# Second token group: stretches without gathers, fewer gathers in its layers, and ten row buffers with the products eight slots behind

## The chip, the cores and the metric

The kernel runs on one core of a Trainium2 chip, as one launch. The metric is the device time of that core in microseconds (us), the median of several runs; lower is better. TensorE is called PE here, VectorE DVE, ScalarE ACT, GpSimd POOL and SyncE SP; each has an instruction queue of its own and works it off in order. A gather is a DMA that POOL issues: it fetches 128 rows of a table, one for each partition, by row numbers that lie in SBUF.

## The reference

512 tokens of width 1024 pass through five layers in a row: a Mamba2 mixer, a sliding-window attention (SWA), a hybrid of gated delta rule and mLSTM, a cross attention to 256 memory tokens, and a PEER expert layer. In the expert layer each token picks, for each of 8 heads, 16 of 16,384 experts; an expert is one row of a table `u` and one row of a table `v`:

```python
q = (hf @ wq).reshape(t, PEER_HEADS, 2, PEER_HALF)
sc = jnp.einsum('thpd,hpnd->thpn', q, sub_keys).astype(jnp.float32)
...
u = jnp.take(u_table, eb, axis=0)
act = jax.nn.gelu(jnp.einsum('phkd,pd->phk', u, xb).astype(jnp.float32), approximate=False)
wgt = (gb * act).astype(v_table.dtype)
return jnp.einsum('phk,phkd->pd', wgt, jnp.take(v_table, eb, axis=0))
```

The layers between the mixers carry matrix products of 1024 by up to 6176, all in float32. Residuals and a last normalization close the chain. Mamba, SWA, the delta rule and the mLSTM go along the tokens, so later tokens need the state of earlier ones.

## The kernel before

The tokens are worked in two groups of 256 (two blocks of 128 each), one group after the other through all layers (`layers`). The expert layer is done in two ways. For the first group the 128 chosen experts of each token are fetched: 2 blocks x 2 tables x 128 slots are 512 gathers of 512 KB each (class `Rows`, line 1928 on). For the second group all 16,384 experts are computed densely on PE in 128 steps (`steps`), each step with a 512 KB tile of the `u` table and one of the `v` table, until the `u` tiles run out after step 93. The dense steps are called the steady expert part below.

The 512 gathers belong to the first group but are not done at its end. They are a side stream, a Python generator (`after`), which `run` (line 1885 on) draws on while it writes down the second group's layers: after each piece of a layer an account grows by a rate of that layer (`RATE`: 1.0 in mamba, 1.1 in SWA, hybrid and cross, 0.5 in the routing), and for each whole unit `Rows.next` writes one gather into the program. What is left when the second group's layers and routing are written goes evenly into the steps of the steady expert part (`steps`, `left`).

`Rows.next` allocates one of 6 row buffers (`gu`), issues the gather on POOL and, once more than `GLAG` = 5 gathers are pending (3 in the steady part), writes the oldest one's product (`take`): one DVE pass over 128x1024 elements, for a `u` row a product with the token that is summed up (L1969), for a `v` row a scaled addition to the output `x` (L1975). A gather thus waits for the product of the gather six before it. `behind` ties each gather and each product, in the order alone, behind the matmul written last.

The order in the queues is a scheduler's. The side stream has a lower priority (-300), and so gathers and products slip to where their engines would be free by the scheduler's reckoning, or pile up behind more urgent work.

Each layer ends alike. The output projection's second half (`out_part`, last=True) is evacuated by DVE (L646), its squares are summed on ACT, mamba and SWA then scale and add (`post`, L607 to L615), and the next layer's `norm_T` needs a power on POOL (L460), a scaling on DVE (L500) and transposes on PE (L412) before the next layer's first matmul can start. Mamba's state update in each chunk goes from POOL (L816) to DVE (L817) to PE. In the hybrid layer `finish` normalizes the heads' output on DVE, ACT and POOL (L1361 to L1378) before it is transposed (`outT`) and projected.

In the second group the weights of these layers are used as float32 as they come (`FULL`), so that the tile `hl` and the tile `ol`, which hold low parts of activations for the first group, have no user in the second group's layers up to the dense part.

Of the kernel before, what the change touches and what calls it, by code (L numbers as in the profile page):

```python
# [9 lines left out]
F32 = mybir.dt.float32  # L10
# [10 lines left out]
D = 1024  # L21
# [125 lines left out]
SPLIT_R = [V]  # L147
SPLIT_D = [V]
SPLIT = {"A": SPLIT_A, "B": SPLIT_B, "R": SPLIT_R, "G": SPLIT_D, "D": SPLIT_D}
RB = 1.0  # L150
RR = 0.5
RT = 1.793
RBS = 1.1
RBH = 1.1
RBX = 1.1
RG = 0.5
RATE = {"A": 0.0, "T": RT, "B": RB, "R": RR, "G": RG, "swa": RBS, "hybrid": RBH, "cross": RBX}
RAWB = 3
# [1 line left out]
GBUF = 6  # L160
HP = 99
WV = (2, 3)
GLAG = 5
GLEAD = 2
GD = 2.9
GU = 0.6
# [20 lines left out]
class Kern:  # L187
    PD = 2

    def __init__(self, ctx, tc, a, out, groups, stop=None):  # L190
# [12 lines left out]
        self.phase = "A"  # L203
        self.tail = None
        self.rows = None
        self.hook = None
        self.tab = ("", [], [])
        self.push("op")
# [271 lines left out]
    def norm_T(self, x, nb, wcol, keep=None, halo=None, ss=None, full=False, dst=None):  # L480
# [4 lines left out]
        with self.tc.high_priority(HP):  # L485
            for b in range(nb):
# [10 lines left out]
                r = self.rstd(s1, 1, "n", 1.0 / D)  # L497
# [7 lines left out]
        with self.tc.high_priority(HP):  # L505
            for k in range(8):
                p = self.ps([128, gt], "tp")
                for b in range(nb):
                    self.tr(p[:, b * 128:(b + 1) * 128], xn[b][:, k * 128:(k + 1) * 128])
                nc.scalar.activation(hh[:, k, :], p, AF.Copy, scale=wcol[:, k:k + 1])  # L510
                if full:
                    continue
                nc.vector.scalar_tensor_tensor(hl[:, k, :], p, wcol[:, k:k + 1], hh[:, k, :].bitcast(F32),
                                               op0=ALU.mult, op1=ALU.subtract)
        if keep is not None:
            for b in range(nb):
                nc.gpsimd.tensor_tensor(keep[0][:, b, :], xn[b], keep[1], op=ALU.mult)
# [100 lines left out]
    def out_part(self, key, oT, nb, kh, k0, evac, last=False, done=None):  # L618
# [8 lines left out]
                yield  # L627
        if last:
            us = [self.W((key, kh, c)) for c in (2, 3)]
            for b in range(nb):  # L630
                for c in (2, 3):
                    p = self.ps([128, 256], "mm")
                    self.n_half(p, us[c - 2], oT, b, k0, True, True)
                    evac(b, c, p)
                    yield
                if done is not None:
                    done(b)
# [403 lines left out]
    def hybrid(self, gi, x, nb):  # L1041
# [317 lines left out]
        oT = self.oT(gt, self.is_full(gi, "ho"))  # L1359

        def finish(b, f0):  # L1361
            fs = slice(f0, f0 + 4)
            if f0 == 4:
                ab = self.sb([128, 4], "dab")
# [33 lines left out]
        yield from self.weave_keep(g_proj("h_z", 0, AF.Silu), side, 2.0)  # L1398
        yield from self.weave(side, ml, 0.5)
        yield from outT(4)  # L1400
        if gi == 0:
            yield from self.memory_kv(2, "cacc", 3)
        fin = chain(*[finish(b, 0) for b in range(nb)], outT(0))
        yield from self.weave(self.out_part("h_o", oT, nb, 1, 4, self.acc_evac(xs)), fin, 1.0)
        self.xss = self.pp.tile([128, nb, 4], F32, name="xss", tag="xss", bufs=2)
        yield from self.out_part("h_o", oT, nb, 0, 0, self.end_evac(xs, self.xss, "P"), last=True)
        if gi == 0:
# [480 lines left out]
    def run(self):  # L1888
# [5 lines left out]
        for gi, (b0, nb) in enumerate(self.groups):  # L1894
            x = self.load_x(gi) if gi else x0
            acc = 0.0
            for _ in self.layers(gi, x, nb):
# [1 line left out]
                if ph == "B" and self.layer in RATE:  # L1899
                    ph = self.layer  # L1900
                acc = min(3.0, acc + RATE[ph])
                while side is not None and acc >= 1:
                    acc -= 1
                    with self.tc.high_priority(GOFF[self.phase] if self.tail is None else TOFF):
                        if next(side, 0) == 0:
                            side = None
# [11 lines left out]
    def after(self, gi, x, nb):  # L1918
# [1 line left out]
        self.tail = None  # L1920
        self.rows = Rows(self, gi, x, nb, self.routed)
        while self.rows.seq:
            self.rows.next(GLAG)
            yield
        self.rows.drain()

# [1 line left out]
class Rows:  # L1928
# [9 lines left out]
    def next(self, lag):  # L1938
# [4 lines left out]
                self.ends.pop(0)  # L1943
        if self.seq:
            b, v, s = self.seq.pop(0)
            t = k.gp.tile([128, D], F32, name="gu", tag="gu", bufs=GBUF)
            table = k.a["p_v" if v else "p_u"]
            self.behind(k.nc.gpsimd.indirect_dma_start(out=t, out_offset=None, in_=table,  # L1948
                                                       in_offset=bass.IndirectOffsetOnAxis(ap=self.res[b][0][:, s:s + 1], axis=0)))
            self.pend.append((b, v, s, t))  # L1950
            if len(self.pend) > lag:
                self.take()
        elif self.pend:
            self.take()

    def behind(self, inst):

# [101 lines left out]
```

## Time and profile before

| what | value |
|---|---|
| median of 3 runs | 2544.5 us (2540.04 to 2547.29) |
| the profiled execution | 2548.39 us, its span 2546.6 us |
| mean granted PE clock, share of full | 0.963 |
| busy PE / DVE / ACT / POOL | 2351.7 / 1983.7 / 1182.3 / 1086.4 us |
| bytes moved by DMA | 642.33 MB, of them 268.47 MB by gathers |

The profile page gives the busy time of each engine over the whole span; the answers to questions to the trace, in the section of rows below, cut it into stretches, and list single instructions with the idle time before them and what ended it (in brackets, "<-"). The granted clock is a share of full speed: 1.00 is 2.4 GHz, 0.5 is 1.2 GHz, and what lies between is a mean over both. The second group's layers run from about 780 to 1640 us, the gathers start at 834 us, routing and the making of the gate matrix follow, and the steady expert part runs from 1893 to 2517 us, with `u` and `v` tiles until 2424 us.

### The profile page before, as it was taken

The page shows a single profiled execution, that of the slowest core. Times are in us where ns is not written, and L with a number is a line of the kernel's source. Part 1 is how long each engine was busy: PE and PEld are TensorE (multiplying, and loading weights), DVE is VectorE, ACT ScalarE, POOL GpSimd, SP SyncE. Part 2 cuts the span into 40 slices and gives each one's busy share as a digit, 9 for nine tenths or more (in the row PEclk, how much of TensorE's full clock was granted, in tenths as well). Part 3 has the DMA queues.
Part 4 walks back from the last instruction along what each step waited for, and adds up shares of the span by engine and source line. Part 5 has one row for each costly group of instructions (what it writes and reads, how often), then busy time and mean ns, then how long its engine had stood idle before and what let it go on. Part 6 is the DMA issues. An engine that isn't in the chain of part 4 may idle for free.

```text
span 2546.6 us, 41073 instructions
## 1 busy us (share of the span) xinstructions
PE 2351.7 (92%) x14872; PEld 2119.6 (83%) x14872; DVE 1983.7 (78%) x3978; ACT 1182.3 (46%) x2450; POOL 1086.4 (43%) x910
## 2 busy tenths in 40 slices
PE   7999998999988989979889967999999999999997
PEld 7999898998888878867768856787999999999974
DVE  7777667757579887877779777699878888888876
ACT  6766566645455433423243222224775444444443
POOL 1111101222010677663648775521225655666663
PEclk9999999999999989989979978999999999999999
DMA  6555534324445899987978769876988898898884
GB/s 205 182 171 156 158 105 151 113 90 128 157 141 173 326 371 342 362 282 258 359 277 285 272 223 393 329 255 207 306 265 321 327 343 307 328 337 324 313 290 157
DMA packets 203962, 642.33 MB, mean 252 GB/s; under 512 B 21104, under 2 KB 53360, under 8 KB 202480
## 3 DMA queue, kind: packets, MB, share of 16 engines
q1 hardware_dynamic: 97216, 347.19, 40.0%
q0 software_dynamic: 73728, 268.47, 29.1%
q10 hardware_dynamic: 32816, 24.06, 3.0%
q8 instruction: 117, 1.92, 0.3%
q14 instruction: 85, 0.70, 0.1%
HBM read 621.74 MB, written 17.89 MB: 251 GB/s over the span
## 4 chain that ended last, share of the span: by engine, by line
PE 61%; DVE 15%; issue 8%; POOL 7%; DMA 5%; ACT 4%; ACTq 0%; POOLq 0%; DVEq 0%; SPq 0%
PE mm L404 37%; PE ax L404 18%; POOL gu L1948 4%; PE tp L404 4%; PE tp L412 3%; DMA gu<-in_p_v,eid 2%; DVE wlo L379 2%; DVE x L1975 2%; DVE cacc L532 1%; DMA gu<-in_p_u,eid 1%; DVE gu L1969 1%; ACT whi L376 1%; DVE wk L1524 1%; DMA gd<-gst 1%; DVE ti L1526 1%
## 5 line engine op out<-in xcount | busy, mean ns | idle before, releaser
L379 DVE TENSOR_TENSOR wlo<-wraw,whi 128x1024 fp32r<-128x1024 f32 x285 | 355.9, 1250 | 170.0 <-ACT whi L376 169.8
L1948 POOL DMA_INDIRECT gu<-in_p_v,eid x256 | 384.2, 1501 | 145.1 <-DVE x L1975 68.6
L1948 POOL DMA_INDIRECT gu<-in_p_u,eid x256 | 312.8, 1222 | 305.9 <-DVE gu L1969 205.4
L404 PE MATMUL mm<-hl,whi 128*128 128x256 f32 (+1 forms) x1376 | 391.6, 285 | 0.0
L376 ACT CAST whi<-wraw 128x1024 fp32r<-128x1024 f32 x285 | 298.9, 1050 | 180.6 <-PE mm L404 85.0
L1975 DVE SCALAR_TENSOR_TENSOR x<-gu,act,x 128x1024 f32<-128x1024 f32 x256 | 341.4, 1333 | 17.1 <-DMA gu<-in_p_v,eid 15.4
L1969 DVE SCALAR_TENSOR_TENSOR gu<-gu,hf 128x1024 f32<-128x1024 f32 x256 | 320.4, 1264 | 33.7 <-DMA gu<-in_p_u,eid 33.3
L404 PE MATMUL mm<-hh,whi 128*128 128x260 f32 (+1 forms) x1232 | 331.4, 343 | 2.7 <-DVE spp L563 1.5
L404 PE MATMUL mm<-hh,wlo 128*128 128x260 f32 (+1 forms) x1200 | 322.7, 340 | 3.9 <-DVE wlo L379 3.9
L404 PEld LDWEIGHTS mm<-hl,whi 128*128 128x128 f32 x1376 | 262.6, 191 | 5.0
L404 PEld LDWEIGHTS mm<-hh,whi 128*128 128x128 f32 x1232 | 235.2, 194 | 21.6 <-ACT hh L510 2.8
L1811 POOL TENSOR_TENSOR w<-act,w 128x256 fp32r<-128x256 f32 x128 | 147.2, 1150 | 240.8 <-issue 181.2
L404 PEld LDWEIGHTS mm<-hh,wlo 128*128 128x128 f32 x1200 | 232.4, 197 | 20.8 <-DVE wlo L379 4.7
L404 PE MATMUL mm<-dhh,wlo 128*128 128x256 f32 x752 | 211.5, 281 | 0.0
L404 PE MATMUL mm<-dhh,whi 128*128 128x256 f32 x752 | 209.8, 279 | 0.0
L404 PE MATMUL mm<-wlo,hh 128*128 128x256 f32 x656 | 176.0, 328 | 0.0
L404 PE MATMUL mm<-whi,hh 128*128 128x256 f32 x608 | 166.8, 328 | 0.4 <-ACT hh L510 0.4
L404 PE MATMUL mm<-whi,oh 128*128 128x256 f32 x560 | 147.4, 327 | 1.7 <-DVE ysb L646 1.1
L1806 ACT CAST w<-act 128x256 fp32r<-128x256 f32 x128 | 52.1, 407 | 208.2 <-DVE act L1804 206.2
L404 PE MATMUL mm<-hh,wraw 128*128 128x256 f32 (+1 forms) x608 | 147.3, 389 | 0.3 <-ACT act L1706 0.3
L404 PEld LDWEIGHTS mm<-dhh,whi 128*128 128x128 f32 x752 | 141.1, 188 | 4.0
L404 PEld LDWEIGHTS mm<-dhh,wlo 128*128 128x128 f32 x752 | 141.2, 188 | 0.0
(494 smaller groups left out, 5610.7 us busy)
## 6 DMA issues: line engine op xcount, KB each, us to landing
wraw<-in_w SPq DMA_DIRECT2D x238, 512.0 KB, 3.8
wraw<-in_p_v SPq DMA_DIRECT2D x78, 512.0 KB, 5.3
wraw<-in_p_ut SPq DMA_DIRECT2D x69, 512.0 KB, 4.7
whi<-in_w SPq DMA_DIRECT2D x55, 512.0 KB, 6.5
wlo<-in_w SPq DMA_DIRECT2D x55, 512.0 KB, 5.9
wrawd<-in_p_v SPq DMA_DIRECT2D x50, 512.0 KB, 5.3
wrawd<-in_p_ut SPq DMA_DIRECT2D x36, 512.0 KB, 4.6
gd<-gst ACTq DMA_DIRECT2D x32, 384.0 KB, 4.9
```

The lines of the kernel that those rows point to most:

```text
L376: nc.scalar.copy(hi, raw)
L379: (nc.gpsimd if le == "P" else nc.vector).tensor_tensor(lo, raw, hi.bitcast(F32), op=ALU.subtract)
L404: inst = self.last = self.nc.tensor.matmul(out, lhsT, rhs, start=start, stop=stop, skip_group_check=True)
L412: return self.nc.tensor.transpose(out, in_, self.ident[:in_.shape[0], :in_.shape[0]])
L532: nc.vector.scalar_tensor_tensor(acc, ps[:, 1 + j:1 + j + gt], w[:, j:j + 1], acc, op0=ALU.mult, op1=ALU.add)
L1524: nc.vector.match_replace(work, ov[:, 0:8], vals, -3.0e38)
L1526: nc.vector.max_index(oi[:, 8:16], ov[:, 8:16], work)
L1806: nc.scalar.copy(wt[:, 0:gt], act)
L1811: nc.gpsimd.tensor_tensor(wt[:, gt:2 * gt], act, wt[:, 0:gt].bitcast(F32), op=ALU.subtract)
L1948: self.behind(k.nc.gpsimd.indirect_dma_start(out=t, out_offset=None, in_=table, in_offset=bass.IndirectOffsetOnAxis(ap=self.res[b][0][:, s ...
L1969: self.behind(nc.vector.scalar_tensor_tensor(t, t, 1.0, self.hf[:, b, :], op0=ALU.mult, op1=ALU.mult, accum_out=acts[b][:, s:s + 1]))
L1975: self.behind(nc.vector.scalar_tensor_tensor(x[:, b, :], t, acts[b][:, s:s + 1], x[:, b, :], op0=ALU.mult, op1=ALU.add))
```

## The change

Three edits act on the side stream, and only while the second group's layers are written.

1. **Quiet stretches.** A flag stops `run` from drawing on the side stream. It is set at the last two column tiles of each layer's output projection and taken back in the next layer's `norm_T`; in the hybrid layer also from the first `finish` to the end of `outT(4)`, and again through the first half of the output projection. The account does not grow beyond 3 meanwhile.
2. **Rates.** Mamba 0.95 for 1.0, SWA 1.15 for 1.1, hybrid 1.05 for 1.1, cross 0.95 for 1.1. What the layers issue less goes to the steady expert part.
3. **Ten row buffers, products eight slots behind.** Four more rows are held in the idle tiles `hl` and `ol`, two in each, and `GLAG` = 5 becomes `DEEP` = 8 in the layers. In the routing it is 5 again, and the first call there takes the surplus.

```diff
-RB = 1.0
+RB = 0.95
...
-RBS = 1.1
-RBH = 1.1
-RBX = 1.1
+RBS = 1.15
+RBH = 1.05
+RBX = 0.95
...
+DEEP = 8
...
         self.rows = None
+        self.quiet = False
         self.hook = None
...
                                                op0=ALU.mult, op1=ALU.subtract)
+        self.quiet = False
         if keep is not None:
...
         if last:
             us = [self.W((key, kh, c)) for c in (2, 3)]
+            self.quiet = True
             for b in range(nb):
...
         def finish(b, f0):
+            self.quiet = gi > 0
             fs = slice(f0, f0 + 4)
...
         yield from outT(4)
+        self.quiet = False
         if gi == 0:
             yield from self.memory_kv(2, "cacc", 3)
         fin = chain(*[finish(b, 0) for b in range(nb)], outT(0))
         yield from self.weave(self.out_part("h_o", oT, nb, 1, 4, self.acc_evac(xs)), fin, 1.0)
+        self.quiet = False
...
-                while side is not None and acc >= 1:
+                while side is not None and acc >= 1 and not (self.quiet and ph != "T"):
...
-            self.rows.next(GLAG)
+            self.rows.next(DEEP if self.phase == "B" else GLAG)
...
-            t = k.gp.tile([128, D], F32, name="gu", tag="gu", bufs=GBUF)
+            t = self.buf()
...
-            if len(self.pend) > lag:
+            while len(self.pend) > lag:
                 self.take()
...
+    def buf(self):
+        k = self.k
+        r = k.rot("rb", GBUF + 4) if k.phase == "B" else 0
+        if r < GBUF:
+            return k.gp.tile([128, D], F32, name="gu", tag="gu", bufs=GBUF)
+        if r % 2 == 0:
+            if r == GBUF:
+                self.pair = k.hp.tile([128, 2, D], F32, name="hl", tag="hl")
+            else:
+                self.pair = k.op_tile([128, 2, D], "ol", "ol")
+        return self.pair[:, r % 2, :]
```

What this does to the queues stands below at three places. A row is a source line, an operation, its output, its inputs, the shape, and a count where rows follow each other alike. The changed file's lines lie a little lower: L460 is L462 there, L650 is L654, L646 is L650, L1948 is L1955, L1969 is L1989.

POOL's queue at the end of mamba, before. `ysb` is the projected output, `pr` and `nr` are the powers for the two normalizations, the DMA rows are gathers:

```order
L650 TENSOR_TENSOR ysb<-ysb,bcw 128x256 x2
L1948 DMA gu<-in_p_u,eid 128x1024
L650 TENSOR_TENSOR ysb<-ysb,bcw 128x256
L1948 DMA gu<-in_p_u,eid 128x1024
L650 TENSOR_TENSOR ysb<-ysb,bcw 128x256
L1948 DMA gu<-in_p_u,eid 128x1024 x4
L460 TENSOR_TENSOR pr<-pv,mhalf 128x1 x2
L913 MEMSET va 128x780
L915 COPY kT<-a_kc 128x4x128
L916 COPY va<-a_vc 128x260
L460 TENSOR_TENSOR nr<-nv,mhalf 128x1 x2
```

The same place on POOL in the changed kernel:

```order
L654 TENSOR_TENSOR ysb<-ysb,bcw 128x256
L1955 DMA gu<-in_p_u,eid 128x1024
L654 TENSOR_TENSOR ysb<-ysb,bcw 128x256
L1955 DMA gu<-in_p_u,eid 128x1024
L654 TENSOR_TENSOR ysb<-ysb,bcw 128x256 x2
L462 TENSOR_TENSOR pr<-pv,mhalf 128x1 x2
L917 MEMSET va 128x780
L919 COPY kT<-a_kc 128x4x128
L920 COPY va<-a_vc 128x260
L462 TENSOR_TENSOR nr<-nv,mhalf 128x1 x2
```

The four gathers ahead of `pr` are gone, and one between the `ysb` rows.

DVE's queue at the end of the hybrid layer, before. The rows `gu,act<-gu,hf` are products of gathered rows, `x<-mm,x` is an evacuation, `ns`, `nv` and `xn` are the cross layer's normalization:

```order
L1969 SCALAR_TENSOR_TENSOR gu,act<-gu,hf 128x1024
L646 TENSOR_TENSOR x<-mm,x 128x256
L1969 SCALAR_TENSOR_TENSOR gu,act<-gu,hf 128x1024
L646 TENSOR_TENSOR x<-mm,x 128x256
L1969 SCALAR_TENSOR_TENSOR gu,act<-gu,hf 128x1024
L496 TENSOR_REDUCE ns_15326<-xss 128x1
L496 TENSOR_REDUCE ns_15335<-xss 128x1
L1969 SCALAR_TENSOR_TENSOR gu,act<-gu,hf 128x1024
L458 TENSOR_SCALAR nv<-ns_15326 128x1
L458 TENSOR_SCALAR nv<-ns_15335 128x1
L1969 SCALAR_TENSOR_TENSOR gu,act<-gu,hf 128x1024
L500 TENSOR_SCALAR xn<-x,nr 128x512 x4
```

The same place on DVE in the changed kernel (`hl` and `ol` are now gathered rows too, L1871 is the last normalization of the first group's first block):

```order
L1989 SCALAR_TENSOR_TENSOR hl,act<-hl,hf 128x1024
L650 TENSOR_TENSOR x<-mm,x 128x256
L1989 SCALAR_TENSOR_TENSOR ol,act<-ol,hf 128x1024 x2
L650 TENSOR_TENSOR x<-mm,x 128x256
L1871 SCALAR_TENSOR_TENSOR gu<-x,finr,gu 128x1024
L650 TENSOR_TENSOR x<-mm,x 128x256 x3
L498 TENSOR_REDUCE ns_15183<-xss 128x1
L498 TENSOR_REDUCE ns_15192<-xss 128x1
L460 TENSOR_SCALAR nv<-ns_15183 128x1
L460 TENSOR_SCALAR nv<-ns_15192 128x1
L502 TENSOR_SCALAR xn<-x,nr 128x512 x4
```

Between the last evacuation and `xn` no product is left. Some products still stand among the evacuations ahead of it.

POOL's queue in the steady expert part, before (`w` is one dense step's weighting, one row for each step):

```order
L1811 TENSOR_TENSOR w<-act,w 128x256
L1948 DMA gu<-in_p_v,eid 128x1024
L1811 TENSOR_TENSOR w<-act,w 128x256
L1948 DMA gu<-in_p_v,eid 128x1024
L1811 TENSOR_TENSOR w<-act,w 128x256
L1948 DMA gu<-in_p_v,eid 128x1024 x2
L1811 TENSOR_TENSOR w<-act,w 128x256
```

The same part in the changed kernel:

```order
L1818 TENSOR_TENSOR w<-act,w 128x256
L1955 DMA gu<-in_p_u,eid 128x1024 x2
L1818 TENSOR_TENSOR w<-act,w 128x256
L1955 DMA gu<-in_p_u,eid 128x1024
L1818 TENSOR_TENSOR w<-act,w 128x256
L1955 DMA gu<-in_p_u,eid 128x1024 x2
L1818 TENSOR_TENSOR w<-act,w 128x256
```

Two gathers come in every second step now, where they came in about every fifth. Counted over POOL's whole queue, the gathers written ahead of each layer's end (the rows `nr` of the next norm) go from 126 to 116 for mamba, from 62 to 61 for SWA, from 104 to 91 for hybrid and from 39 or 40 to 28 for cross; between there and the first `w` row they go from 54 or 55 to 57; behind it from 126 to 159.

## Rows read from the trace of the kernel before

**Rows 1.** Windows: busy us (instructions) by engine, clock, DMA share; line one names columns.

```profile
core 0: us, PE busy (x) PEld busy (x) DVE busy (x) ACT busy (x) POOL busy (x), PEclk, DMA share, GB/s
840.00:1100.00 260.00, 240.01 (x1217) 212.44 (x1217) 215.25 (x399) 94.64 (x226) 185.45 (x153) 0.93 0.96 356
1100.00:1140.00 40.00, 24.55 (x117) 20.34 (x116) 28.41 (x82) 13.45 (x35) 25.07 (x25) 0.79 0.76 259
...
1260.00:1300.00 40.00, 24.78 (x107) 20.29 (x108) 28.30 (x50) 12.62 (x36) 23.20 (x22) 0.79 0.74 263
...
1480.00:1520.00 40.00, 17.61 (x80) 14.76 (x81) 32.37 (x77) 8.88 (x22) 35.27 (x31) 0.66 0.55 180
1520.00:1540.00 20.00, 17.78 (x82) 13.93 (x80) 14.52 (x28) 2.41 (x6) 11.98 (x11) 1.00 1.00 383
1540.00:1560.00 20.00, 8.42 (x37) 6.34 (x36) 15.83 (x34) 3.56 (x14) 13.59 (x13) 0.79 0.98 380
1560.00:1640.00 80.00, 76.32 (x352) 64.54 (x351) 58.24 (x129) 20.70 (x64) 45.29 (x40) 0.97 0.96 364
...
1893.00:2424.00 531.00, 531.00 (x3408) 481.74 (x3407) 439.09 (x406) 254.81 (x381) 316.58 (x210) 1.00 0.88 322
...
400.00:420.00 20.00, 13.43 (x91) 12.35 (x90) 12.47 (x25) 9.40 (x23) 2.56 (x4) 0.83 0.48 152
```

**Rows 2.** Timeline of PE, after its long waits: start, us, [idle before].

```profile
947.94 0.69 PE L404 MATMUL ax<-m_h,abc 128*128 128x64 f32 x2 [6.21 <-DVE m_h L817]
...
1119.59 0.66 PE L412 MATMUL tp<-ident,xn 128*128 128x128 f32 x2 [14.05 <-DVE xn L500]
...
1280.98 0.66 PE L412 MATMUL tp<-ident,xn 128*128 128x128 f32 x2 [13.71 <-DVE xn L500]
...
1503.63 0.69 PE L412 MATMUL tp<-ident,mixed 128*128 128x128 f32 x2 [11.40 <-DVE mixed L1378]
...
1510.87 0.66 PE L412 MATMUL tp<-ident,mixed 128*128 128x128 f32 x2 [6.55 <-DVE mixed L1378]
...
1559.04 1.39 PE L412 MATMUL tp<-ident,xn 128*128 128x128 f32 x4 [10.30 <-DVE xn L500]
...
1639.16 0.41 PE L412 MATMUL tp<-ident,xn 128*128 128x128 f32 x2 [2.90 <-DVE xn L500]
1641.07 0.69 PE L412 MATMUL tp<-ident,xn 128*128 128x128 f32 x2 [1.50 <-DVE xn L500]
```

**Rows 3.** Timeline of POOL at the end of mamba.

```profile
1106.10 0.98 POOL L1948 DMA_INDIRECT gu<-in_p_u,eid  x1 [0.16 <-issue]
...
1111.26 0.59 POOL L460 TENSOR_TENSOR pr<-pv,mhalf 128x1 f32<-128x1 f32 x1
```

**Rows 4.** Timeline of DVE at the end of the hybrid layer.

```profile
1557.26 1.23 DVE L1969 SCALAR_TENSOR_TENSOR gu<-gu,hf 128x1024 f32<-128x1024 f32 x1 [1.75 <-DMA gu<-in_p_u,eid]
...
1558.41 1.67 DVE L500 TENSOR_SCALAR xn<-x,nr 128x512 f32<-128x512 f32 x4
```

**Rows 5.** Timeline of DVE in mamba, ahead of PE's wait at 947.94.

```profile
945.92 1.23 DVE L1969 SCALAR_TENSOR_TENSOR gu<-gu,hf 128x1024 f32<-128x1024 f32 x1 [2.58 <-DMA gu<-in_p_u,eid]
...
947.47 0.41 DVE L817 TENSOR_TENSOR m_h<-ax,m_h 128x256 f32<-128x256 f32 x1
```

**Rows 6.** Waits from 830 to 1900: who for whom, us, times, longest.

```profile
POOL gu L1948 <- DVE gu L1969: 210.7, 85, 15.0
```

**Rows 7.** Groups by line on DVE, 1893 to 2424: busy us, mean ns, idle.

```profile
L1975 DVE SCALAR_TENSOR_TENSOR x<-gu,act,x 128x1024 f32<-128x1024 f32 x110 | 147.6, 1342 | 0.7
```

**Rows 8.** Timeline of DVE in a dense step with two products.

```profile
2109.83 2.96 DVE L1975 SCALAR_TENSOR_TENSOR x<-gu,act,x 128x1024 f32<-128x1024 f32 x2
2112.71 1.21 DVE L379 TENSOR_TENSOR wlo<-wrawd,whi 128x1024 fp32r<-128x1024 f32 x1
```

**Rows 9.** The gathers' line, 1893 to 2424: duration ns min/median/max; time to landing.

```profile
L1948 POOL DMA_INDIRECT gu<-in_p_v,eid x114: 942/1764/1952, 1893.8 to 2422.6; - x114
...
DMA to landing us min/median/max: 4.9/7.2/12.0
```

## The prediction

> **What bounds the kernel now.** I read the windows first, stage by stage, then the timeline of PE for what stands ahead of its long waits, then the timelines of DVE and POOL at those places. Over the span PE is the engine with the most work, but not everywhere for the same reason. In the steady expert part PE is busy for 531.00 of 531 us at a clock of 1.00 [rows 1]; there only more work on PE, or PE being starved, changes the time. In the second group's layers PE waits for chains that run over DVE and POOL. At the end of mamba it stands still for 14.05 us, at the end of SWA for 13.71, in the hybrid layer's `finish` for 11.40 and 6.55, before cross for 10.30, before the routing for 2.90 and 1.50 [rows 2]. The clock pays again: the stretches around those gaps have 0.79, 0.79, 0.66 and 0.79 [rows 1]. What ended each wait is DVE, and what DVE and POOL did meanwhile is the side stream. At the end of mamba POOL's power for the normalization, `pr`, runs at 1111.26, behind gathers issued from 1106.10 on [rows 3]. At the end of the hybrid layer DVE, which goes in order, waits 1.75 us for a gather to land, multiplies for 1.23 us, and only then does the `xn` that PE needs [rows 4]. In mamba a product that waits 2.58 us for its gather stands before `m_h` on DVE, and PE waits 6.21 us for `m_h` [rows 2, 5]. POOL in turn waits 210.7 us for products that free a row buffer [rows 6]. The DMA engines are the third party: 0.96 busy in mamba at 356 GB/s and 0.96 in cross at 364, but 0.88 at 322 in the steady part [rows 1].
>
> **Part by part.** The sum is made against the profiled execution, 2548.4 us, which is 3.9 us above the median of 2544.5.
>
> *The quiet stretches.* A layer that ends with scaling and adding (mamba, SWA) keeps, without gathers, the chain evacuation, squares, `pr`, scaling, norm, `xn`, transpose. In mamba's rows `pr` issues at 1111.26 and could have issued when the gathers began at 1106.10, about 5 us earlier; one or two products of 1.23 us [rows 5] leave DVE's part. I take 6.5 us back of 14.05 and 6 of 13.71. The bounds are 3 (only POOL's part counts, and less of it) and 9 (the rest as short as before the routing). For hybrid to cross the nearest row is the gap before the routing, 2.90 + 1.50 = 4.4 us, the same chain with fewer products in it: 10.30 - 4.4 = 6 us; bounds 3 and 8. For `finish` the queue still has seven products in the changed kernel where ten stood, since they come eight slots late; three times 1.23 is 3.7 us, and POOL's powers and multiplications have fewer gathers before them. I take 6 of the 17.95 us; bounds 0 and 10. The hybrid layer's output projection, 1510.87 to 1548.7, loses PE at the rate of the window 1520 to 1540, 2.22 us in 20, which is 4.2 us; I take 4, bounds 0 and 6.
>
> *The clock after those gaps.* A stretch at clock c loses (1 - c) times its busy time: 0.21 x 24.55 = 5.2, 0.21 x 24.78 = 5.2, 0.34 x 17.61 = 6.0 and 0.21 x 8.42 = 1.8, together 18.2 us [rows 1]. That a shorter gap still costs some is shown by the first group, where the 20 us from 400 on have a clock of 0.83 with 13.43 us busy, 2.3 us lost [rows 1]. Four of those leave 18.2 - 9.2 = 9; I take 8, bounds 3 and 12.
>
> *Rates and depth in mamba and cross.* Ten gathers leave mamba (126 to 116) and eleven or twelve leave cross. In mamba PE idles for 260 - 240 = 20 us and loses 0.07 x 240 = 16.8 us to the clock [rows 1]. Those waits come from products that wait for their gathers [rows 5], and a product eight slots behind finds its row landed more often than one five behind. But mamba can't shrink below its transfers: ten gathers of 0.524 MB are 5.24 MB, at 356 GB/s 14.7 us [rows 1]. So the bounds are 0 (DVE is in order, and some product will stand before `m_h` anyway) and 14.7; I take 10, nearer to the upper end because the loss that can go, 37 us, is over twice the cap. In cross PE idles 80 - 76.3 = 3.7 us; I take 2, bounds 0 and 3.7. SWA and hybrid keep their density, and I cost the buffers at nothing there: what hides a longer queue is DMA engines that were 0.74 to 0.76 busy around the layer ends; if that cover is gone, a tile comes some us late once for each end. Two rows of a pair share a tile, so the first gather of a pair waits for two products, the later of which was written just before it: no slack for 2 in 10 gathers, against none for all of them now [rows 6].
>
> *The drop from eight to five in the routing* writes three surplus products in one call, 3 x 1.23 = 3.7 us on DVE; I take 2, bounds 0 and 4.
>
> *The steady expert part* takes 33 more gathers, 28 of them until 2424 us (a step with a `u` tile counts double in `steps`: 186 of 216 parts). DVE has 439 us of work in 531, and 28 x 1.342 = 38 us make it 477, or 90% [rows 1, 7]. POOL goes from 317 us by 28 x 1.764 = 49 to 366, 69% [rows 1, 9]. PE gets nothing. A step with two products exists already: both ran from 2109.83, the next weight split followed at 2112.71 without idle [rows 8], and PE is at 531.00 with it. Such steps go from about one in five to one in two. The transfers are the tight part: 322 GB/s x 531 us = 171 MB, plus 28 x 0.524 = 14.7 MB makes 185.7 MB, and 350 GB/s in the same time. The lower bound is zero, since mamba sustains 356. The upper bound is that 322 is all this mixture gives: 185.7 / 0.322 = 577, or 46 us. Gathers land after 7.2 us, at most 12.0 [rows 9]; three slots behind was 2.5 steps of 5.6 us (531 / 94), 14 us, and is now 2 steps, 11.2 us, so a few late ones now hold DVE. I take 4 us, near zero, because mamba's rate covers the need.
>
> The Trainium skill has a rule that speaks against this edit. In "DMA: Bandwidth & Descriptors", section "Where 436 GB/s comes from", it says that for transfers between HBM and SBUF the HBM side binds at about 358 GB/s for one core. The mamba window agrees, 356 over 260 us, and the window 1520 to 1540 shows 383 for a short while. By that rule the steady part would run at 98% of the limit and cost nothing but late landings, as taken here; by the section's other figure, 425 measured with one large transfer, there would be room.
>
> The sum: 6.5 + 6 + 6 + 6 + 4 + 8 + 10 + 2 = 48.5 less 2 and 4 is 42.5 us. 2548.4 - 42.5 = 2505.9, and 3.9 less as a median: **2502 us**.
>
> **Rivals.**
>
> *Half of it comes back (about 2526).* Products already in the queue slide into the quiet stretches, as the order shows in `finish` and among the hybrid evacuations, the clock falls at each gap as in the first group, and mamba stays at its transfers. With the lower bounds of the gaps (3 + 3 + 3 + 0), clock 3, mamba 10 and cross 1 it is 23, less 5 for the steady part and routing: 18 us, so 2544.5 - 18 = 2526. For it: DVE is 0.83 busy in mamba. Against it: between the last evacuation and `xn` nothing is left.
>
> *The eight slots do more (about 2478).* With all upper bounds of gaps, clock, mamba and cross (9 + 9 + 10 + 8 + 6 + 12 + 14.7 + 3.7 = 72) and 6 back, it is 2544.5 - 66 = 2478. Against it: that all ends are reached at once.
>
> *The steady part becomes like mamba (slower, about 2585).* There DMA engines at 0.96 and DVE at 0.83 go with a PE that has 240 of 260 us at 0.93, 0.86 of full rate [rows 1]. The steady part would have 0.88 x 350 / 322 = 0.96 and 0.90. At 0.86 its 531 us become 617, 86 more; the layers give 46.5, so the kernel loses 40. It decides from the point where PE falls below 92% of full rate there, 46 us. For it: the same two shares. Against it: PE waits there for weights split a step ahead, and not for `m_h` behind a product.
>
> *It doesn't do what it says:* the scheduler could put gathers into the quiet stretches. The order excludes that for POOL at the ends.
>
> **How the numbers follow.** What a measurement can tell from no change is about 0.3%, 7.6 us: faster is below 2537, slower above 2552. The forecast with its own range, 2486 to 2518, has 0.55; the eight slots that do more 0.12; half 0.16, of it 0.02 above 2537; no change through a steady part that eats the gain (its 46 us bound) 0.08; the steady part like mamba 0.09. Faster is 0.55 + 0.12 + 0.14 = 0.81, same 0.10, slower 0.09. The range that leaves out 2 in 10 goes from 2474 to 2538.
>
> **What would show it.** Right: PE's waits before `xn` at the ends of mamba and SWA near 7 us, before cross near 4, clocks around them above 0.85; `pr` on POOL straight after its input; fewer waits of PE for `m_h`; the steady part still some 624 us long with PE at 1.00 and DMA near 350 GB/s. Wrong: idle PE or a clock below 1.00 in the steady part, or gaps as long as before with products in them.

## The result, and the profile after

The changed kernel takes 2507.42 us (median of 4 runs, 2503.7 to 2515.05) against 2545.89 us of the kernel before on the same chip (4 runs, 2540.04 to 2549.67): ratio 0.9847 with a 95% interval of 0.9829 to 0.9865. That is 38.5 us by the medians. The forecast was 2502 us, the range 2474 to 2538. The profiled execution of the changed kernel took 2507.27 us, its span 2505.5 us.

The windows of the changed kernel that answer to [rows 1]. Stages end earlier now, so the stretches are moved along: mamba, the ends of mamba, SWA and `finish`, the evacuations ahead of cross, the steady part as far as the `u` tiles go, and the step from the first group.

```profile
core 0: us, PE busy (x) PEld busy (x) DVE busy (x) ACT busy (x) POOL busy (x), PEclk, DMA share, GB/s
830.00:1080.00 250.00, 239.54 (x1250) 212.57 (x1249) 211.31 (x394) 97.72 (x232) 183.15 (x148) 0.96 0.95 360
1080.00:1120.00 40.00, 30.65 (x145) 25.72 (x144) 30.86 (x89) 13.25 (x40) 24.54 (x24) 0.87 0.70 241
1230.00:1270.00 40.00, 32.31 (x145) 27.09 (x144) 26.66 (x50) 14.12 (x41) 22.46 (x23) 0.87 0.86 332
1445.00:1485.00 40.00, 21.81 (x103) 18.46 (x104) 28.80 (x61) 8.40 (x20) 33.30 (x28) 0.70 0.56 174
...
1495.00:1515.00 20.00, 13.14 (x56) 10.60 (x55) 12.87 (x29) 5.32 (x19) 10.95 (x10) 0.82 0.92 322
1844.00:2372.00 528.00, 524.83 (x3376) 475.32 (x3375) 458.29 (x459) 246.21 (x377) 334.79 (x235) 1.00 0.93 346
```

Two things are to be seen. The stretches at the stage ends have more work in 40 us at a higher clock, but the one at `finish` (1445 to 1485) hardly. And in the steady part PE, which was at 531.00 of 531, is at 524.83 of 528: it waits.

The timeline of PE in the changed kernel, after its long waits, answering to [rows 2].

```profile
1099.89 0.45 PE L414 MATMUL tp<-ident,xn 128*128 128x128 f32 x1 [7.95 <-DVE xn L502]
...
1250.58 0.66 PE L414 MATMUL tp<-ident,xn 128*128 128x128 f32 x2 [6.22 <-DVE xn L502]
...
1468.31 0.69 PE L414 MATMUL tp<-ident,mixed 128*128 128x128 f32 x2 [12.94 <-DVE mixed L1383]
...
1472.11 0.66 PE L414 MATMUL tp<-ident,mixed 128*128 128x128 f32 x2 [3.11 <-DVE so L1378]
...
1510.68 1.39 PE L414 MATMUL tp<-ident,xn 128*128 128x128 f32 x4 [6.46 <-DVE xn L502]
```

The timeline of the changed kernel at the end of mamba shows that the reason that [rows 3] gave is gone: POOL's `pr` starts after an idle 0.97 us, straight behind its input, with no gather queued ahead.

```profile
1089.66 0.15 DVE L460 TENSOR_SCALAR pv<-pss 128x1 f32<-128x1 f32 x1
...
1089.89 0.57 POOL L462 TENSOR_TENSOR pr<-pv,mhalf 128x1 f32<-128x1 f32 x1 [0.97 <-DVE pv L460]
```

The stages side by side, from one profiled execution each (start of the named matmul or POOL operation, us; the sums of stages of two executions can differ by some us by themselves):

| stage, up to | before | after | the stage's change |
|---|---|---|---|
| first group and mamba, first `xn` transpose of SWA | 1119.59 | 1099.89 | -19.7 |
| SWA, first transpose of hybrid | 1280.98 | 1250.58 | -10.7 |
| hybrid, first transpose of `mixed` | 1503.63 | 1468.31 | -4.9 |
| second transpose of `mixed` | 1510.87 | 1472.11 | -3.4 |
| projection, first transpose of cross | 1559.04 | 1510.68 | -9.6 |
| cross, first transpose of the routing | 1641.07 | 1591.36 | -1.4 |
| routing, first steady matmul of `dhh` | 1896.86 | 1844.54 | -2.6 |
| steady part, last `dhh` matmul (`u` tiles end) | 2420.26 | 2372.10 | +4.2 |
| steady part, last `w` on POOL | 2527.76 | 2489.31 | +9.7 |
| end of the span | 2546.6 | 2505.5 | -2.6 |

The first gather starts at 833.99 us before and at 835.00 after; counted from there, mamba gives 20.7 us. The layers and the routing give 52 us. The steady part takes 13.9 of them back and the tail returns 2.6. The waits of DVE in the changed kernel between the start of the steady part and the last `w` (us, times, longest) show what the kernel before did not have there: products wait for their gathers, 44.7 and 10.3 us.

```profile
DVE x L1995 <- DMA gu<-in_p_v,eid: 44.7, 36, 6.0
...
DVE gu L1989 <- DMA gu<-in_p_u,eid: 10.3, 8, 4.7
```

One such wait in the timeline of the changed kernel, on DVE and then on PE: the product at 2303.32 waited 5.95 us for its row, the weight splits queued behind it ran late, and PE stood 1.71 us for `wlo`.

```profile
2303.32 1.29 DVE L1995 SCALAR_TENSOR_TENSOR x<-gu,act,x 128x1024 f32<-128x1024 f32 x1 [5.95 <-DMA gu<-in_p_v,eid]
2304.52 2.35 DVE L381 TENSOR_TENSOR wlo<-wrawd,whi 128x1024 fp32r<-128x1024 f32 x2
...
2305.79 0.96 PE L406 MATMUL ax<-wlo,w 128*128 128x512 f32 x3 [1.71 <-DVE wlo L381]
```

The waits and the loss do not fall in the same place. All but at most 3.2 us of the waits for gathers lie ahead of 2372 us, where the steady part lost 4.2 us; 9.7 us were lost behind the last `u` tile. The windows of that last stretch, before and after, have PE idle for 3.7 us and for 9.9:

```profile
2420.30:2527.80 107.50, 103.84 (x407) 72.02 (x407) 79.85 (x82) 44.28 (x67) 56.70 (x47) 1.00 0.67 234
```

```profile
2372.10:2489.30 117.20, 107.29 (x406) 72.24 (x405) 89.47 (x91) 45.56 (x69) 65.85 (x53) 0.99 0.73 257
```

PE waits there for weight splits. That DVE came into this stretch late from the waits ahead of it is the likely reason, but no trace shows the delay being carried over.

### The profile page after: what moved, and what is told of

Read it like the earlier page. It is cut to its first block, busy times and chain, and to the rows that moved or that the text cites. A ratio compares the mean times of both kernels' runs of the same rounds, so it can differ in the third digit from the quotient of the medians.

```text
span 2505.5 us, 40945 instructions
## 1 busy us (share of the span) xinstructions
PE 2346.4 (94%) x14872; PEld 2117.7 (85%) x14872; DVE 1975.4 (79%) x3978; ACT 1177.5 (47%) x2451; POOL 1075.9 (43%) x910
## 4 chain that ended last, share of the span: by engine, by line
PE 63%; DVE 14%; DMA 8%; issue 7%; POOL 4%; ACT 4%; ACTq 0%; DVEq 0%; POOLq 0%; SPq 0%
PE mm L406 41%; PE ax L406 16%; DMA gu<-in_p_v,eid 4%; PE tp L414 3%; DVE wlo L381 3%; PE tp L406 3%; DVE x L1995 2%; POOL gu L1955 1%; DVE cacc L535 1%; ACT whi L378 1%; DMA gd<-gst 1%; DVE act L1811 1%; DMA ol<-in_p_v,eid 0%; DVE xn L502 0%; DVE wk L1531 0%
## 5 line engine op out<-in xcount | busy, mean ns | idle before, releaser
L1955 POOL DMA_INDIRECT gu<-in_p_u,eid x190 | 250.2, 1317 | 245.7 <-DVE gu L1989 162.0
L1955 POOL DMA_INDIRECT gu<-in_p_v,eid x206 | 297.5, 1444 | 68.8 <-issue 33.1
L1995 DVE SCALAR_TENSOR_TENSOR x<-gu,act,x 128x1024 f32<-128x1024 f32 x206 | 272.3, 1322 | 48.4 <-DMA gu<-in_p_v,eid 45.2
L1989 DVE SCALAR_TENSOR_TENSOR gu<-gu,hf 128x1024 f32<-128x1024 f32 x190 | 239.4, 1274 | 17.0 <-DMA gu<-in_p_u,eid 14.5
```

What stands on the lines that cost most here:

```text
L1989: self.behind(nc.vector.scalar_tensor_tensor(t, t, 1.0, self.hf[:, b, :], op0=ALU.mult, op1=ALU.mult, accum_out=acts[b][:, s:s + 1]))
L1995: self.behind(nc.vector.scalar_tensor_tensor(x[:, b, :], t, acts[b][:, s:s + 1], x[:, b, :], op0=ALU.mult, op1=ALU.add))
```

## The experiments

Every kernel was timed beside the kernel before on one chip, and ratios are to that. "Four slots" below means that `LAGD`, the number of pending gathers in the steady part, is 4 and not 3.

### Is the steady part's loss a matter of the distance between gather and product?

**Four slots in the changed kernel:**

```diff
-LAGD = 3
+LAGD = 4
```

> The changed kernel with products four slots behind in the steady part instead of three. The steady part got 14 us longer from its first weighting to its last, and DVE waits there 55 us for gathers that have not landed. If the distance is too short for 1.5 gathers a step, those waits go below 15 us and the steady part gets 5 to 9 us shorter: ratio to before about 0.982 instead of 0.985. If the DMA engines are simply full there, the waits stay in another place and the ratio stays 0.985.

Measured: 2492.15 us (5 runs, 2492.1 to 2492.78), ratio 0.9785 (0.9764 to 0.9806). The steady part, first `dhh` matmul to last `w`, went from 644.8 to 632.6 us, against 630.9 before the change: 12.1 us less, where 5 to 9 had been expected. DVE's wait for gathers there fell from 55 us to the 4.1 of the waits' row below, and the window under it has PE busy all the time, with the same moved gathers.

```profile
DVE x L1995 <- DMA gu<-in_p_v,eid: 4.1, 4, 1.5
```

```profile
1842.00:2365.00 523.00, 523.00 (x3371) 474.92 (x3370) 468.10 (x461) 252.05 (x377) 362.92 (x236) 1.00 0.95 351
```

So neither the volume (351 GB/s here, more than the 346 of the slower version) nor DVE's load (468 us busy) set the time: it was one slot of distance. How much the short distance costs varies, though: two versions below with as many moved gathers and three slots (rates alone and without depth) have steady parts of 637.5 and 638.8 us, with 49.7 and 44.8 us of such waits. The four versions with four slots and 21 to 55 moved gathers lie at 632.2 to 634.7. The gathers' line in this kernel, 1842 to 2365 us, shows them landing after 5.2, 8.4 and 14.2 us (least, median, most), where 4.9, 7.2 and 12.0 stood [rows 9]:

```profile
L1955 POOL DMA_INDIRECT gu<-in_p_v,eid x110: 937/1765/1967, 1967.5 to 2363.8; - x110
...
DMA to landing us min/median/max: 5.2/8.4/14.2
```

**The same edit in the kernel before:**

> The kernel before with one edit: in the steady part products run four slots behind their gathers in place of three. Theory A: the wait of VectorE for gathers in the steady part arises only through the moved gathers (before the change VectorE's wait there is under 1 us), so the ratio is 0.998 to 1.002 and the steady part stays at 629 to 632 us. Theory B: four slots shorten the steady part by themselves, as the u tiles' part of 523.4 us did not but the later part might (107.5 us before): 622 to 627 us, ratio 0.996 to 0.998.

Measured: 2551.56 us, ratio 1.0002 (0.9986 to 1.0019), the steady part 630.9 us. Theory A holds: the distance of three was enough for the gathers of before, about 1.2 in a step with a `u` tile, and became too short through the moved ones.

### What each part does alone

**Quiet zones alone**, at rates that leave as many gathers ahead of the steady part as before (387 by the trace, 386 before), six buffers, five slots:

```diff
-DEEP = 8
+DEEP = 5
...
-        r = k.rot("rb", GBUF + 4) if k.phase == "B" else 0
+        r = 0
...
-RB = 0.95
-RBS = 1.15
-RBH = 1.05
-RBX = 0.95
+RB = 1.035
+RBS = 1.16
+RBH = 1.2
+RBX = 1.36
```

> Quiet stretches alone, with six buffers and five slots, and the rates raised to 1.035, 1.16, 1.2 and 1.36 so that the same number of gathers stays in each layer as in the kernel before (126, 62, 103, 39) and the steady part keeps its 126. If the gaps at the layers' ends are the main term (their working: 28 us of gaps and evacuations, 8 of clock), it is 20 to 36 us faster than before: some of it goes back because the rest of each layer is denser, so I take 22 us, ratio 0.991. If only the volume that leaves the layers counts, nothing has left, and the ratio is 1.000. If the depth is what counts, 1.000 as well.

Measured: 2533.78 us, ratio 0.9947 (0.9929 to 0.9965): 14.7 us by the medians, less than the 20 to 36 expected. The gaps at the ends of mamba and SWA shrank to 8.24 and 7.23 us, but mamba as a whole, from the first gather to SWA's first transpose, took 285.6 us as before: with the same number of gathers in the rest of the layer, what the gap gave went back there.

**Lower rates alone** (0.92, 1.08, 0.96, 0.79 in mamba, SWA, hybrid, cross; 352 gathers), without quiet zones, six buffers, five slots; the quiet zones go by

```diff
-                while side is not None and acc >= 1 and not (self.quiet and ph != "T"):
+                while side is not None and acc >= 1:
```

> No quiet stretches, six buffers, five slots, but lower rates (0.92, 1.08, 0.96, 0.79), so that each layer gives up as many gathers as in the changed kernel (116, 61, 94, 26) and the steady part gets 160. If the volume counts, it brings most of the 38 us: ratio about 0.987. If the gaps count, they stay, as products still stand before the norms: mamba and cross give back about 10 us, the steady part costs its 12, so 1.000 within 0.003.

Measured: 2531.48 us, ratio 0.9933 (0.9911 to 0.9954). That lies between the two expectations, 0.987 and 1.000 within 0.003, so neither is borne out.

**Depth alone** (ten buffers, eight slots; rates of before, no quiet zones; 386 gathers):

> Ten buffers and eight slots alone, with the rates of before and no quiet stretches. If late gathers that hold DVE are a main term in the layers, mamba's waits for m_h shrink and it is 10 us or more faster, ratio 0.996 or below. If the gaps at the layers' ends are the main term, they stay, and a later product may even fall into them: ratio 0.997 to 1.003.

Measured: 2523.87 us, ratio 0.9913 (0.9893 to 0.9933): the first case, though the gaps at the two ends stand as before (14.24 and 12.40 us). PE's waits for `m_h` fell from 19.1 to 12.3 us.

### What is lost when one part is left out

**Without quiet zones** (the one line above in the changed kernel):

> The changed kernel with the quiet zones taken out; lower rates and ten buffers with eight slots stay (373 gathers before the steady part against 351 in the change and 387 before it). Theory A: the waits of TensorE at the stage boundaries (14.05 and 13.71 us before, 7.95 and 6.22 us in the change) are the quiet zones' alone, since neither lower rates alone (11.70, 14.07) nor depth alone (14.24, 12.40) shortened them. Then they stand again at 11 to 14 us each, the layers are some 12 us longer, the steady part with 14 moved gathers some 8 us shorter than in the change, and the ratio is 0.986 to 0.990. Theory B, the three parts mend the same late gathers: the boundary waits stay under 9 us without quiet zones, and the ratio is 0.981 to 0.984.

Measured: 2522.28 us, ratio 0.9902 (0.9886 to 0.9918). The ratio is a little above theory A's range. Its timeline of PE has the waits at the ends of mamba and SWA back, as theory A said, and the longest one of all at `finish`. But this version also has 20 gathers more ahead of the steady part than the change (373 against 353), so the 22 us by which its layers are longer are not the quiet zones' alone:

```profile
1104.85 0.66 PE L414 MATMUL tp<-ident,xn 128*128 128x128 f32 x2 [13.98 <-DVE xn L502]
...
1266.43 0.66 PE L414 MATMUL tp<-ident,xn 128*128 128x128 f32 x2 [11.91 <-DVE xn L502]
...
1491.51 0.69 PE L414 MATMUL tp<-ident,mixed 128*128 128x128 f32 x2 [21.23 <-DVE mixed L1383]
```

**Without depth** (`DEEP` 5, six buffers in the changed kernel):

> The changed kernel with six row buffers and products five slots behind, as before; quiet zones and lower rates stay (353 gathers before the steady part). Theory A, the parts add up: depth alone gained 24.6 us (ratio 0.9913 by medians), so without it the ratio is 0.993 to 0.996. Theory B, lower rates and depth mend the same late gathers: the waits of VectorE's products for gathers are nearly gone through the lower rates too, and the ratio is 0.985 to 0.990. The steady part (start of the steady part to the last output row) is as in the change, about 645 us, by both.

Measured: 2519.71 us, ratio 0.9892 (0.9876 to 0.9908), in theory B's range. But its reason is not borne out: DVE still waits 34.2 us for gathers in the layers, of 48.7 before. And the steady part took 638.8 us, where both theories had about 645.

**Without the lower rates** (1.0, 1.1, 1.1, 1.1 again):

> The changed kernel with the rates of before; quiet zones and depth stay (365 gathers before the steady part, so 22 moved and not 36). Theory A, that gathers in the steady part cost by their number: the steady part is 14 x 22/36 = 8.5 us longer than before (about 639 us), the mamba and cross stages are 4 to 8 us longer than in the change, ratio 0.984 to 0.987. Theory B, that the 36th gather is what makes the steady part late (a threshold): it is at 631 to 634 us, and the ratio is 0.980 to 0.983.

Measured: 2505.55 us, ratio 0.9828 (0.9811 to 0.9846), steady part 634.6 us. Its interval overlaps that of the change, so leaving the rates out cost nothing that can be told at three slots: the layers are 9.7 us longer and the steady part is 10.2 us shorter.

The six together. Two readings are PE's waits for `xn` at the ends of mamba and SWA, and DVE's waits for gathers from 830 to 1640 us (all rows of that kind added). "Layers" goes from the first gather to the first steady matmul, with the routing, and "steady" from there to the last `w`, each in one execution. Three pairs of versions that do not differ ahead of the steady part show how far "layers" scatters: 1062.9 and 1066.4 (before), 1019.3 and 1024.0 (without rates), 1009.5 and 1008.9 (the change), each with three and four slots.

| kernel | ratio | PE at the two ends, us | DVE for gathers, us | layers, us | steady, us | gathers ahead of the steady part |
|---|---|---|---|---|---|---|
| before | 1 | 14.05, 13.71 | 48.7 | 1062.9 | 630.9 | 386 |
| quiet zones alone | 0.9947 | 8.24, 7.23 | 48.9 | 1045.2 | 634.3 | 387 |
| rates alone | 0.9933 | 11.70, 14.07 | 33.3 | 1039.8 | 637.5 | 352 |
| depth alone | 0.9913 | 14.24, 12.40 | 23.1 | 1038.7 | 633.6 | 386 |
| without quiet zones | 0.9902 | 13.98, 11.91 | 8.5 | 1031.7 | 632.0 | 373 |
| without depth | 0.9892 | 7.67, 7.54 | 34.2 | 1019.8 | 638.8 | 353 |
| without rates | 0.9828 | 8.26, 6.78 | 12.8 | 1019.3 | 634.6 | 365 |
| the change | 0.9847 | 7.95, 6.22 | 9.1 | 1009.5 | 644.8 | 353 |

The first column of waits falls to 8.3 us or less with the quiet zones, and nothing else moves it by more than 2.4; the second moves with depth and, less, with the rates. For the second, DVE's waits for gathers in the kernel with quiet zones alone, and below them in the one with depth alone (us, times, longest; `hl` and `ol` hold the added buffers):

```profile
DVE gu L1989 <- DMA gu<-in_p_u,eid: 32.9, 33, 3.3
...
DVE x L1995 <- DMA gu<-in_p_v,eid: 16.0, 19, 2.3
```

```profile
DVE ol L1989 <- DMA ol<-in_p_u,eid: 8.6, 7, 2.9
...
DVE gu L1989 <- DMA gu<-in_p_u,eid: 7.5, 8, 2.2
...
DVE hl L1989 <- DMA hl<-in_p_u,eid: 7.0, 7, 1.8
```

So quiet zones and depth mend different waits: alone they gave 0.53% and 0.87%, and together, without the lower rates but with 21 gathers fewer in the layers, 1.72%. Rates and depth mend the same one: alone they gave 0.67% and 0.87%, together (without quiet zones) 0.98%.

### Do the rates pay when the steady part has room, and is there room for more?

**Rates of before, four slots:**

> The changed kernel with the rates of before (365 gathers before the steady part, 12 more than with the change's rates) and with products of the steady part four slots behind. Theory A: the lower rates did earn time in the layers and only lost it in the steady part (the steady part starts 9 us later without them, 1853.8 against 1844.5 us), so once four slots remove the loss, the version without them is the slower: 0.982 to 0.984 against 0.9785 with them, the steady part 631 to 633 us in both. Theory B: the lower rates earn nothing by themselves, quiet zones and depth do it all: 0.977 to 0.980.

Measured: 2508.18 us, ratio 0.9839 (0.9819 to 0.986), steady part 632.2 us. Theory A: with four slots the lower rates are worth 0.0054, about 14 us (the layers alone 15.1, 1024.0 against 1008.9), and this version is no better with four slots (0.9839) than with three (0.9828): its steady part had lost only 3.7 us to begin with (634.6 against 630.9).

**Lower rates once more, four slots** (0.90, 1.05, 0.95, 0.85; 331 gathers):

> The changed kernel with four slots in the steady part and the layer rates lowered again (0.95, 1.15, 1.05, 0.95 to 0.90, 1.05, 0.95, 0.85): 22 more gathers move to the steady part (331 before it). Theory A: the steady part still has room, since TensorE is busy 499.5 of 500 us there and the DMA share is 0.95; the layers are 8 to 14 us shorter, the steady part 0 to 4 us longer: ratio 0.974 to 0.977. Theory B: the transfers are at their limit; 22 gathers of 0.524 MB at 353 GB/s are 32.7 us of transfer against 5% of 632 = 32 us of room, so part of it shows, the steady part is 10 us or more longer: ratio 0.979 or more.

Measured: 2496.02 us, ratio 0.9782 (0.9758 to 0.9805): not to be told from 0.9785 with 353. Both theories missed. Theory B's 10 us are not there, the steady part took 634.7 us; and the window of its part with `u` tiles has 369 GB/s with PE at 524.00 of 524:

```profile
1846.00:2370.00 524.00, 524.00 (x3376) 475.81 (x3376) 488.52 (x501) 250.16 (x378) 396.57 (x254) 1.00 0.98 369
```

But the layers got no shorter either: 1007.7 us against 1008.9 in the version with 353. The stages did move. Mamba, from the first gather on, gave 4.0 us (262.1 against 266.1), and hybrid up to the second transpose of `mixed` took 9.2 more (227.8 against 218.7), with PE's waits at `finish` at 12.06 and 5.86 us. Taken as a whole, fewer gathers spread evenly no longer shortened the layers at 353; why hybrid grew stays open.

**An earlier quiet zone in the hybrid layer, four slots** (342 gathers):

```diff
+        self.quiet = gi > 0
         yield from self.weave(side, ml, 0.5)
```

The reason to try it stood in the timeline of DVE in the changed kernel: among `finish`'s small steps, between 1450.92 and 1473, stand seven products of 1.25 us from slots ahead of the zone (with four slots in the steady part eight, from 1448 to 1474). Three of them:

```profile
1456.74 1.25 DVE L1995 SCALAR_TENSOR_TENSOR x<-hl,act,x 128x1024 f32<-128x1024 f32 x1
1457.91 0.15 DVE L1378 TENSOR_TENSOR so<-so,cf 128x4 f32<-128x4 f32 x1
...
1460.12 1.27 DVE L1995 SCALAR_TENSOR_TENSOR x<-hl,act,x 128x1024 f32<-128x1024 f32 x1
1461.32 0.16 DVE L460 TENSOR_SCALAR ov<-so 128x4 f32<-128x4 f32 x1
...
1461.48 1.25 DVE L1995 SCALAR_TENSOR_TENSOR x<-ol,act,x 128x1024 f32<-128x1024 f32 x1
...
1467.31 0.16 DVE L1382 TENSOR_TENSOR cf<-cf,or 128x4 f32<-128x4 f32 x1 [2.85 <-POOL or L462]
```

> The changed kernel with four slots in the steady part, and the hybrid's quiet zone of the second group begun ahead of the mLSTM part and not at the first finish: 11 more gathers move to the steady part (342 before it). Theory A: TensorE's wait at the finish (12.92 + 3.11 us with four slots) is the eight products of 1.25 us that stand on VectorE among the finish's small steps, with gathers between them on GpSimd, both from slots ahead of the zone. With the earlier zone they are gone by then, the wait falls to 5 to 8 us together, the stage to 8 us less, the steady part stays within 3 us of 632.6: ratio 0.974 to 0.977. Theory B: the wait is the finish's own chain through three engines (reduce, scale, power on GpSimd, scale again): still 12 us or more, ratio 0.978 to 0.981.

Measured: 2479.44 us (5 runs, 2476.86 to 2481.87), ratio 0.9726 (0.9709 to 0.9744): the fastest version here. Its timeline of PE, after the waits at `finish` and ahead of cross:

```profile
1454.92 0.69 PE L414 MATMUL tp<-ident,mixed 128*128 128x128 f32 x2 [5.39 <-DVE mixed L1383]
...
1461.03 0.66 PE L414 MATMUL tp<-ident,mixed 128*128 128x128 f32 x2 [5.42 <-DVE mixed L1383]
...
1496.04 0.41 PE L414 MATMUL tp<-ident,xn 128*128 128x128 f32 x2 [3.02 <-DVE xn L502]
```

The ratio is below the range of theory A. The wait at `finish` is 10.8 us where 16.0 stood. Theory A said 5 to 8; no product runs on DVE and no gather is issued on POOL from 1435 to 1463 us, so these 10.8 are `finish`'s own chain, as theory B had it for all. Up to the second transpose of `mixed` the stage is 8.1 us shorter (218.67 to 210.56), and the steady part took the 11 further gathers with 633.2 us. Another 3.8 us came back ahead of cross, for a reason told below. Eleven gathers taken from this one place were worth more than the 22 taken evenly.

## Why the prediction was right, and where it was not

*The sum.* 42.5 us were forecast for the profiled execution, 41.1 came (38.5 by the medians). But the agreement is partly luck: layers and routing gave 52 where 46.5 stood, and the steady part with the tail took 11 where 4 stood. Idle PE in the steady part, which the prediction named as a sign of being wrong, is there.

*Gaps between layers.* At the end of mamba 6.1 us came back (forecast 6.5), of SWA 7.5 (6), ahead of cross 3.8 (6). For the first two the reason held: without quiet zones they stand at 13.98 and 11.91. Ahead of cross it did not. The prediction said that the order keeps gathers out of POOL's queue at the ends; at the end of hybrid one is left, and it waits for its row buffer, which an output transfer still reads, right in front of the power `nr` that the chain needs:

```profile
1508.47 0.94 POOL L1955 DMA_INDIRECT gu<-in_p_u,eid  x1 [5.67 <-DMA out<-gu]
1509.44 1.13 POOL L462 TENSOR_TENSOR nr<-nv,mhalf 128x1 f32<-128x1 f32 x2
```

DVE waits 4.39 us for this `nr`. With the earlier zone no gather stands there, `nr` follows its input, and the gap is 3.02 us. But it is 2.70 in the changed kernel without quiet zones too, so this gap depends on what happens to stand in the queues there and not on the zones alone.

*`finish`.* The step that failed: "I take 6 of the 17.95 us". It gave 1.9 (12.94 + 3.11 = 16.05). The seven products are there as counted, but the three that were to go did not leave the stretch that PE waits for: between the first step of `finish` on DVE (1488.45 before, 1453.89 after) and the second transpose of `mixed` six products run before and six after. The zone begins where their slots have already been written. With the earlier zone, in which no product stands in that stretch, 5.2 us of the wait went and 8.1 of the stage.

*The clock after the gaps.* Also a failed term: 8 us forecast. By the windows the loss is 0.13 x 30.65 + 0.13 x 32.31 + 0.30 x 21.81 + 0.18 x 13.14 = 17.1 us, against 18.2 before: 1 us. More work came into those stretches at a higher clock, so what is lost to the clock stays nearly as large. Windows that begin at the first transpose behind the gap say the same: the 40 us from there on have 0.94 after mamba and 0.89 after SWA, before and after the change alike. The clock paid in mamba, where the prediction had it within the 10 us of the next term: 0.96 where 0.93 stood, 0.04 x 239.5 = 9.6 us lost in 250 against 16.8 in 260.

*Rates and depth.* 10 us were taken for mamba; the stage gave 19.7 less the gap's 6.1, so 13.6, inside the bound of 14.7. PE's waits for `m_h` fell from 19.1 to 10.2 us. In SWA and hybrid the prediction put the buffers at nothing ("I cost the buffers at nothing there"): wrong. SWA gave 3.2 us beside its gap, the hybrid layer 6.5 ahead of `finish`'s wait, and depth alone, which leaves the gaps at the ends of mamba and SWA as they are, gave 0.9913 and shortened SWA by 3.5 us and hybrid up to the first transpose of `mixed` by 9.7. DVE's waits for rows were spread over the layers and not only in mamba: 19.3 us there, 11.7 in SWA, 3.7 in hybrid, 14.1 from the projection to the end of cross. For hybrid that is too little to be all of the cause: 13 of its 104 gathers left it too, which the prediction did not count, and rates alone shortened it by 5.1 us. What depth does there stays open. The output projection gave 5.8 (4), from 37.9 to 32.1 us, cross 1.4 (2).

*The routing* was to cost 2 us for the surplus products and gave 2.6; no experiment bears on that.

*The steady part* was the mis-sized term: +4 taken, +13.9 measured, -2.6 in the tail. The passage named the right mechanism, "now 2 steps, 11.2 us, so a few late ones now hold DVE", but put too low a price on it. With landings of up to 12.0 us before and 14.2 in the kernel with four slots, 11.2 us of distance was short for 44 products and not for a few. Four slots took 12.1 us of the 13.9 back. The rival "steady part like mamba" fell: PE never came near 0.86 of full rate, and at four slots even 22 gathers more cost it 2 us.

The Trainium skill gives, in "DMA: Bandwidth & Descriptors", section "Where 436 GB/s comes from", about 358 GB/s as the limit of the HBM side for one core, worked out as half of a stack's 716 GB/s. In this trace, of a kernel that runs on one core, it did not bind: 369 GB/s were moved over 524 us in the version with the most gathers moved, 193 MB, and PE did not wait. By the page's figure these would take 193 / 0.358 = 540 us, an estimate, 16 more than they took.

## What to carry to other kernels

When work that prefetches is moved to another stage, the distance between fetch and use has to be recounted there in microseconds: the same number of slots is less time where more fetches go into a step, and landings came later where more was moved (a median of 8.4 us at 351 GB/s, 7.2 at 322). A stretch kept free for a chain has to begin as many slots ahead of it as are in flight, or the uses already queued still stand in it; and one prefetch that waits for its buffer can hold the chain behind it in its engine's queue. At the start quiet zones and thinning were worth about the same (0.53% and 0.67%); once both and the depth were there, keeping one more chain free gave 0.6% and thinning evenly once more nothing. Leaving one part out of the whole told more than adding up the parts alone.

## What the runs showed of the hardware

Not expected was what one slot does: 346 GB/s and 55 us of waits with three slots, 351 GB/s and 4 us with four, all else the same. With 33 or 34 moved gathers the three versions with three slots wait 45 to 55 us; at four slots even 55 moved gathers leave 16.0. And the transfers had more room than the sum allowed: 361 GB/s over 524 us in the version with the earlier zone and 369 in the one with 331 gathers in the layers, where 356 to 364 were the highest sustained rates in the kernel before [rows 1].

What stays open: why the routing gained 2.6 us, how the steady part's waits come to cost most behind the last `u` tile, and how much of the stages' differences within one execution is scatter. The version with the rates of before ended mamba at 1107.36 us with three slots and at 1114.52 with four, though the two do not differ in the layers. Of these 7.2 us, 3.6 arose ahead of the first gather (834.56 and 838.14) and 3.6 in mamba; so a stage's length from one execution may be off by about 4 us and its end by 7, and only the ratios carry the verdicts.
